# One load of seven rows in place of six rows and a row cut over 126 and 2 partitions, in a softmax kernel

## The chip, the cores and the metric

The kernel runs on one core of a Trainium2 chip. The metric is the device time in microseconds. The profile gives the span from the first to the last instruction, which is about 1.4 us shorter than the time.

## The reference

```python
x_scaled = x / 2.0                                   # x: 16 x 1024 x 512, float32
x_max = np.max(x_scaled, axis=-1, keepdims=True)
exp_x = np.exp(x_scaled - x_max)
return exp_x / np.sum(exp_x, axis=-1, keepdims=True)
```

So 16,384 rows of 2,048 bytes are read once and written once: 33.55 MB each way.

## The kernel before

Each of the 128 partitions gets 128 rows, in ten tiles of 3, 7, 13 and then seven times 15 rows. VectorE (DVE) takes the maximum of each row, ScalarE (ACT) the exponential with its sum, VectorE the reciprocal and the product, all in place in one arena. The first tile is loaded from SyncE's (SP) queue, all others from ScalarE's; the stores go out on SyncE's queue. I count tiles from 0 as the code does and call tile 1 the second tile, tile 2 the third.

```python
PLAN = [
    ([3], 0), ([4, 3], 3), ([5, 4, 4], 10), ([5] * 3, 23), ([5] * 3, 38), ([5] * 3, 53),
    ([5] * 3, 68), ([5] * 3, 83), ([5] * 3, 0), ([5] * 3, 15),
]
# ...
SPREAD = 1
# ...
FUSED = {1, 2, 3}
# ...
            if t == 0:
                nc.sync.dma_start(out=sb(t), in_=dram(xf, t)).then_inc(ld[t], 16)
            elif t == SPREAD:
                r = tiles[t][1] - 1
                for p, q, lo, hi in ((0, P, 0, r), (0, 126, r, r + 1), (126, P, r, r + 1)):
                    nc.scalar.dma_start(
                        out=sb(t)[p:q, lo:hi], in_=dram(xf, t)[p:q, lo:hi]
                    ).then_inc(ld[t], 16)
            else:
                nc.scalar.dma_start(out=sb(t), in_=dram(xf, t)).then_inc(ld[t], 16)
# ... (cut) the stores, one per tile, when its last product is done
        for t in range(len(tiles)):
            nc.sync.wait_ge(s_mul, last_chunk[t] + 1)
            nc.sync.dma_start(out=dram(of, t), in_=sb(t)).then_inc(
                st[t] if t in awaited else s_end, 16
            )
```

The second tile thus comes in three DMAs: six rows of all partitions, then the seventh row of partitions 0 to 125, then that of the last two. Below, *split* is this cut over 126 and 2 partitions. A *semaphore packet* is a 4-byte packet, which stands in the trace's packet strings after an engine's rows of a DMA. There are 336 here, which is 16 for each of 20 DMAs and 16 for the two of the split together. The second tile is waited for with 48 increments: 32 updates of its semaphore come from 7.35 us on, as many as its semaphore packets, and two updates at 1.30 and 1.65 us make up the rest. The *pair* are the two DMA engines whose strings hold no 2,048-byte packet, so no row of the split; the bytes that the pair is spared are its *relief*.

## Time and profile before

| | before |
|---|---|
| time, median of the first three runs | 160.04 us (159.99 to 160.07) |
| span of the profile | 158.6 us |
| DVE, ACT busy | 83%, 60% |
| DMA packets, moved | 3,026, 67.13 MB, mean 423 GB/s |
| landing of the second tile, third tile, last load | 9.25, 16.96, 127.64 us |
| issue of the last store, its landing | 146.98, 158.61 us |

How to read it: the 16 DMA engines have work all the time, while VectorE waits only for a handful of landings. The view of waits gives the whole idle time of VectorE for loads; the columns are total us, number of waits, longest.

```profile
DVE stats L118 <- DMA arena<-in_x_dram: 14.6, 5, 6.2
```

Four of these five waits matter here: for tiles 0, 1 and 2 (6.22, 1.30 and 2.37 us) and, near the end, for the last load (3.29 us).

### The profile page before, as it was taken

Reading aid. Unit: us, or ns where it says so; the run is one execution under the profiler, and the core shown is the slowest. Engines: PE = TensorE matmul, PEld = TensorE weight load, DVE = VectorE, ACT = ScalarE, POOL = GpSimd, SP = SyncE. Lnnn points to the kernel's source line nnn. Section 1 sums busy time; section 2 is a strip of 40 time slices with the busy share of each in tenths; the row PEclk is TensorE's granted clock in tenths of the full one; section 3 lists DMA queues with packets and bytes.
Section 4 is the critical chain, followed back from the end, with each engine's and each line's share of the span. In section 5 each row is a group of like instructions: output and inputs, shape, how many; then the busy total and the mean of one; then the engine's idle time right before and its main releaser. Section 6 shows DMA issues by size and latency. Waiting matters only on the chain.

```text
span 158.6 us, 621 instructions
## 1 busy us (share of the span) xinstructions
DVE 131.4 (83%) x155; ACT 94.4 (60%) x257; POOL 0.2 (0%) x4
## 2 busy tenths in 40 slices
DVE  0466799999999999999999999996999389999000
ACT  0369197736874594669738797666566809763000
POOL 0000000000000000000000000000000000000000
DMA  7999999999999999999999999999999999999996
GB/s 268 449 373 430 414 431 466 435 407 399 466 443 389 434 463 448 418 444 426 442 426 434 426 426 442 426 441 411 457 395 472 395 473 395 472 395 465 395 472 263
DMA packets 3026, 67.13 MB, mean 423 GB/s; under 512 B 336, under 2 KB 336, under 8 KB 720
## 3 DMA queue, kind: packets, MB, share of 16 engines
q1 hardware_dynamic: 1584, 34.34, 50.6%
q10 hardware_dynamic: 1440, 32.77, 48.5%
q14 instruction: 2, 0.02, 0.0%
HBM read 33.55 MB, written 33.55 MB: 423 GB/s over the span
## 4 chain that ended last, share of the span: by engine, by line
DMA 52%; DVE 38%; issue 0%
DMA arena<-in_x_dram 38%; DVE stats L118 18%; DMA out_dram<-arena 14%; DVE arena L131 13%; DVE arena L138 7%; DVE recip L127 1%
## 5 line engine op out<-in xcount | busy, mean ns | idle before, releaser
L118 DVE TENSOR_REDUCE stats<-arena 128x5 f32<-128x2560 f32 (+2 forms) x27 | 72.2, 2676 | 14.6 <-DMA arena<-in_x_dram 14.6
L176 ACT ACTIVATE arena<-arena,stats 128x512 f32<-128x512 f32 x68 | 48.2, 710 | 23.4 <-DVE stats L118 23.4
L211 ACT ACTIVATE arena<-arena,stats x60 | 42.5, 710 | 20.7 <-ACTq L203 20.7
L138 DVE TENSOR_SCALAR arena<-arena,recip 128x512 f32<-128x512 f32 x93 | 38.6, 482 | 0.7
L131 DVE TENSOR_TENSOR arena<-arena,recip 128x2560 f32<-128x2560 f32 (+2 forms) x8 | 19.9, 2491 | 0.3
L176 ACT ACTIVATION_READ_ACCUMULATOR arena<-arena,stats 128x1 f32 x68 | 12.7, 187 | 0.0
L211 ACT ACTIVATION_READ_ACCUMULATOR arena<-arena,stats x60 | 11.2, 187 | 0.0
L127 DVE RECIPROCAL recip<-stats 128x5 f32<-128x5 f32 (+2 forms) x27 | 4.8, 177 | 0.0
L171 ACT ACT_TABLE_LOAD x1 | 1.3, 1283 | 5.7 <-issue 5.7
L252 POOL MEMSET const-bfloat16-1.0<- 128x1 bf16 x1 | 0.1, 101 | 0.0
L252 POOL MEMSET const-uint8-127<- 128x1 uint8 x1 | 0.1, 101 | 0.0
L252 POOL MEMSET const-float32-0.0<- 128x1 f32 x1 | 0.1, 98 | 0.2 <-issue 0.2
L252 POOL MEMSET const-float32-1.0<- 128x1 f32 x1 | 0.1, 98 | 0.0
## 6 DMA issues: line engine op xcount, KB each, us to landing
arena<-in_x_dram ACTq DMA_DIRECT2D x7, 3840.0 KB, 46.6
out_dram<-arena SPq DMA_DIRECT2D x7, 3840.0 KB, 22.7
arena<-in_x_dram ACTq DMA_DIRECT2D x1, 3328.0 KB, 14.3
out_dram<-arena SPq DMA_DIRECT2D x1, 3328.0 KB, 21.1
out_dram<-arena SPq DMA_DIRECT2D x1, 1792.0 KB, 18.2
arena<-in_x_dram ACTq DMA_DIRECT2D x1, 1536.0 KB
arena<-in_x_dram SPq DMA_DIRECT2D x1, 768.0 KB, 6.2
out_dram<-arena SPq DMA_DIRECT2D x1, 768.0 KB, 15.8
```

The source lines that it names most:

```text
L118: nc.vector.reduce_max(out=stats[:, b : b + c], in_=arena[:, a : a + c], axis=mybir.AxisListType.X, negate=True,)._wait_ge(ld[t], 48 if t ...
L127: nc.vector.reciprocal(out=recip[:, b : b + c], in_=stats[:, b : b + c])._wait_ge(s_exp, k + 1).then_inc(s_rec, 1)
L131: nc.vector.tensor_mul(out=arena[:, a : a + c], in0=arena[:, a : a + c], in1=recip[:, b : b + c].unsqueeze(2).to_broadcast([P, c, D]),)._w ...
L138: ins = nc.vector.tensor_scalar_mul(out=arena[:, a + r], in0=arena[:, a + r], scalar1=recip[:, b + r : b + r + 1],)
L171: nc.scalar.preload_act_table(mybir.ActivationFunctionType.Exp)
L176: ins = nc.scalar.activation(out=arena[:, a + r], in_=arena[:, a + r], func=mybir.ActivationFunctionType.Exp, bias=stats[:, b + r : b + r ...
L211: ins = nc.scalar.activation(out=data, in_=data, func=mybir.ActivationFunctionType.Exp, bias=stat, scale=0.5, accum_out=stat,)
L252: nc = _bacc.Bacc("TRN2", target_bir_lowering=False, num_devices=1)
```

## The change

Its intent is to drop the special case: the second tile becomes one DMA of seven rows, with rows no longer dealt unevenly to the DMA engines.

```diff
-SPREAD = 1
...
-            elif t == SPREAD:
-
-                r = tiles[t][1] - 1
-                for p, q, lo, hi in ((0, P, 0, r), (0, 126, r, r + 1), (126, P, r, r + 1)):
-                    nc.scalar.dma_start(
-                        out=sb(t)[p:q, lo:hi], in_=dram(xf, t)[p:q, lo:hi]
-                    ).then_inc(ld[t], 16)
...
-        )._wait_ge(ld[t], 48 if t == SPREAD else 16).then_inc(s_max, 1)
+        )._wait_ge(ld[t], 16).then_inc(s_max, 1)
```

## The prediction

> **What bounds the kernel now.** I read the page first. VectorE (DVE) is the busiest compute engine at 83%, so it is no full bound, and ScalarE (ACT) at 60% is less. The row that matters is the DMA row of the 40 slices: nine tenths or more in every slice but the first and the last. In the queue table, q1 (the stores, and the first load) and q10 (all other loads) together fill 99.1% of sixteen engines' span.
>
> ```profile
> span 158.6 us, 621 instructions
> DVE 131.4 (83%) x155; ACT 94.4 (60%) x257; POOL 0.2 (0%) x4
> DMA  7999999999999999999999999999999999999996
> q1 hardware_dynamic: 1584, 34.34, 50.6%
> q10 hardware_dynamic: 1440, 32.77, 48.5%
> HBM read 33.55 MB, written 33.55 MB: 423 GB/s over the span
> ```
>
> The chain that ended last agrees only in part. It runs through DVE for 38% of the span, and that must not be taken as "DVE bounds it": the queues held enough work for the DMA engines while DVE was on the chain. Its start is what the change touches: the landing of the 13-row third tile at 16.96 us, then DVE without a pause.
>
> ```profile
> DMA 52%; DVE 38%; issue 0%
> 2.65 14.32 DMA arena<-in_x_dram
> 16.99 2.82 DVE stats L118
> 81.49 46.15 DMA arena<-in_x_dram
> 127.66 2.82 DVE stats L118
> ```
>
> Because DMA is full, the next question is which of the 16 engines ends last. The profile's views do not name the engine of a packet, but the trace has the start, duration, size and queue of each. A packet starts about 3.5 ns before the recorded end of the one before it on its engine, and each engine must see the same sequence (8 rows of each tile, then one 4-byte semaphore packet). With those two rules I joined all 3,024 data and semaphore packets into 16 gapless strings; the only pauses over 50 ns are two of 0.30 us, at the 8,192-byte instruction fetches at 28.1 and 71.3 us. This assignment is mine, an inference from times. Twelve strings contain nine 2,048-byte packets, two contain ten and two none, as the split demands. The two without are the last to end. What a window count can confirm of that: from 0 to 1.4 us 14 packets start, one on each of 14 engines; the other two engines start at 1.73 and 1.75 us. From 157.4 to 158.0 us 14 engines send their last semaphore packet; only from 158.05 us on do the last two.
>
> ```profile
> q1 hardware_dynamic: 14, 0.09, 35.5%
> ...
> q1 hardware_dynamic: 14, 0.00, 1.3%
> ...
> q1 hardware_dynamic: 2, 0.00, 0.5%
> ```
>
> (In order: windows 0 to 1.4, 157.4 to 158.0 and 158.05 to 158.3 us; the first figure is packets.) In my strings the fourteen engines with split rows end between 157.49 and 157.95 us, and the two without at 158.15 and 158.20. So the kernel ends when the two engines end that carry 18 KB less than the rest: 0.25 us after the next one, and 0.6 after most. They start about 0.5 us late and lose another half microsecond on stretched packets between 30 and 150 us.
>
> [...] the tile's semaphore got two early increments (1.30 and 1.65 us, by count the 2 + 14 that no engine sends) and 32 = 16 + 14 + 2 others from 7.35 to 9.25 us. [...] (from 18.3 us on, 6,144-byte stores alternate with 30,720-byte loads).
>
> **The change, part by part.**
>
> The view of issues by line has what goes:
>
> ```profile
> L110 ACTq DMA_DIRECT2D arena<-in_x_dram x3: 244/386/664, 0.1 to 1.2; - x3
> arena<-in_x_dram ACTq DMA_DIRECT2D x1, 252.0 KB
> arena<-in_x_dram ACTq DMA_DIRECT2D x1, 4.0 KB
> ```
>
> 1. Two issues on ACT's queue go: 3 x 431 ns on average become one, so about 0.9 us of sequencer time. They lie before the first ACT instruction that waits on data (8.01 us), and the next load is needed by an engine only when the second tile's packets are through (about 7.7 us). Worth nothing at the end.
> 2. Work of each engine. From the packet records: 12,288 B take 460 ns, 14,336 B take 535 (the stores of this very tile have that size), 2,048 B take 84, a semaphore packet 9; less the overlap of 3.5 each. Before, an engine of the fourteen spends 8 x 456.5 + 9 x 80.5 + 5.5 = 4,382 ns on this tile (its first semaphore packet is on both sides), the two that have the odd rows 86 more, and the last two 8 x 456.5 = 3,652. Afterwards all spend 8 x 531.5 = 4,252. So twelve engines save 0.13 us, two save 0.22, and the two slow ones get 0.60 more.
> 3. What lies on the path: the end is the maximum over engines. The fourteen fall to 157.3 to 157.8 us, which buys nothing. The two slow ones go from 158.15 and 158.20 to 158.75 and 158.80. The last landing was 0.42 us after the last semaphore packet (158.61), hence about 159.2: +0.60 us.
> 4. The tile lands earlier: without the burst of small packets, whose increments arrive up to 1.0 us after their packets, it should land near 8.40 + 0.45 = 8.85 us instead of 9.25 (0.45 is that delay at the third tile; 8.40 is the slow engines' 7.79 + 0.60). DVE waited 1.30 us there and waits 2.37 us again at 16.99 for the third tile, which comes 0.2 to 0.3 later. The early gain is swallowed by the later wait.
> 5. The tail on DVE: from the last load's landing (127.64) to the last store's issue (146.98) is 19.34 us. If the landing slips 0.6, so does the issue, to 147.6; with the 1.0 us from issue to first packet seen at the start, packets at 148.6. The slow engines finish the preceding store at 149.1 + 0.6, so they never starve; the quick ones may pause 0.3 us, inside their slack.
>
> Sum on the path: +0.60 us, all from step 3.
>
> **The rivals.**
>
> - *The late start comes from the split.* The two late engines start at 1.73 us, just after the last of ACT's three issues ended (1.48) and its immediate increments (1.65). If the three issues held up the first load's last two engines, removing them gives back up to 0.5 us and the time is about 160.15. For: the coincidence. Against: the first load is issued before all of them on another queue, and the two slow engines lose as much again after 30 us with no split in sight. I give it one in four.
> - *The gain in issues and in small packets counts.* If the fourteen engines set the end, the time would fall by 0.13 us to 159.9. Against: the last two semaphore packets are 0.2 us behind the rest, and 0.6 behind most.
> - *Changed order of traffic.* The first store may be issued about 0.4 us earlier and so interleave with other loads; with whole 30,720-byte packets (1.14 us) as the unit, landings can move by a packet. The store tail has 1.1 us of slack on the slow engines (149.1 against 148.0), so most of this stays hidden; if a landing slipped by two packets, 161.0 to 161.5 would come out.
> - *All DMA-bound engines even out.* If the stretched packets come from sharing with each other, a slower pair runs with fewer competitors at the end and regains some: +0.3, so 160.35.
>
> **Range and chances.** +0.60 is the plain sum, 160.64; the first and the last rival pull below it, the third above, and I take 160.6. The low end is the first rival (160.1), the high end a further half microsecond of stretched packets on the slow pair (161.1). Two per cent is 3.2 us, five times the effect, with runs of before within 0.1 us of each other: faster 1%, same 98%, slower 1%.
>
> **What would show it.** Right: 320 semaphore packets instead of 336 and no 2,048-byte ones (under 8 KB 576 = 320 + 256 instead of 720); one issue at that line; the same 14 packets before 1.4 us; 14 last semaphore packets at 157.3 to 157.9 us and two near 158.8; second tile's first reduction at 8.8 to 8.9 us and the third's near 17.2. Wrong: 16 packets before 1.4 us (first rival); the last semaphore packets within 0.3 us of each other; a DMA slice below nine tenths in the middle, or a wait of DVE after 130 us, which would mean that the order of traffic decides.

## The result

The changed kernel took 160.25 us (median of four runs, 159.98 to 160.38), the kernel before 160.06 in the same rounds (159.99 to 160.15). Executions over 1.5% slower than the fastest of the same kernel are left out of the means. Here and below a ratio is the mean time of one kernel's runs over that of the other's runs of the same rounds, so it is not quite the ratio of the medians quoted. It is 1.001, with a 95% interval of 0.9992 to 1.0027: no change that these runs can tell from zero, inside the predicted range, and well short of the +0.60 us of the sum.

The page of the changed kernel, lines that answer to those of before:

```profile
span 158.8 us, 619 instructions
DMA  7999999999999999999999999999999999999995
DMA packets 2882, 67.13 MB, mean 423 GB/s; under 512 B 320, under 2 KB 320, under 8 KB 576
```

The DMA row is as full as before. The packet counts are those predicted: 16 semaphore packets and 128 packets of 2,048 bytes are gone. Now the chain that ended last (start us, us, what):

```profile
1.59 14.86 DMA arena<-in_x_dram
...
16.47 2.82 DVE stats L110
...
81.33 46.90 DMA arena<-in_x_dram
...
128.25 2.82 DVE stats L110
```

Two starts are to be compared with those in the prediction. The third tile's reduction starts at 16.47 us instead of 16.99: 0.52 us earlier, where I had said 0.2 to 0.3 later. The last load's reduction starts at 128.25 instead of 127.66: 0.59 us later, as said. The gain of half a microsecond at 16 us is gone, and more, at 128 us. Where it goes is seen best in the windows view. Its columns are the window, its length, busy time and count of DVE, ACT and POOL, PE's clock, the DMA share, and GB/s by the packets that start in it. First before, then changed:

```profile
6.00:14.00 8.00, 6.44 (x6) 5.66 (x14) 0.00 (x0) 1.00 1.01 404
14.00:50.00 36.00, 33.42 (x21) 23.05 (x64) 0.00 (x0) 1.00 1.01 433
```

```profile
6.00:14.00 8.00, 7.06 (x7) 5.35 (x15) 0.00 (x0) 1.00 1.04 449
14.00:50.00 36.00, 33.30 (x21) 22.68 (x63) 0.00 (x0) 1.00 1.01 420
```

The share of busy DMA engines is full in all four; only the rate differs. Without the split the DMA engines move 449 GB/s between 6 and 14 us instead of 404, and then 420 instead of 433 for 36 us. As busy and moving less, the engines have stretched packets here; the table below has how much.

From the packets I rebuilt the sixteen strings again and took each engine's *lag*: the time of day less the time that its packets so far would have taken unstretched. Mean lag gained over the 16 engines, in us (not a view of the profile; the mean needs no strings, since the packets' times beyond the usual time of their size, summed and divided by 16, give the same within 0.04 us):

| kernel | 5 to 14 us | 14 to 60 us | 60 to 130 us |
|---|---|---|---|
| before | 0.56 | 0.30 | 0.06 |
| changed | 0.01 | 1.08 | 0.05 |

So the change takes away a stall of about half a microsecond on *all* engines near 8 us, which I had not expected, and gets as much and more back before 60 us. In the kernel before, 0.45 of the 0.56 us falls on 16 packets, the first of the third tile on each engine (1,341 to 1,485 ns where 987 is usual), and only 0.02 on the 2,048-byte packets themselves: the DMA that is cut looks normal, and the one behind it pays. What comes back has a place too. Between 14 and 25 us the engines lose, by the same sum, 0.36 to 0.51 us in each of the seven profiles of this text without an early stall, and 0.02 in each of the seven with one.

The window counts of the last semaphore packets (from 157.4 to 158.0, and from 158.05 to 158.3 us; the first figure is packets) answer to the 14 and 2 of before:

```profile
q1 hardware_dynamic: 10, 0.00, 0.9%
...
q1 hardware_dynamic: 5, 0.00, 1.1%
```

No pair stands alone any more: five engines end in the later window, and one more after it, at 158.44 us. The two engines that I took for last should have ended at 158.75 and 158.80.

### The profile page after: what moved, and what is told of

It reads as the page before. It is cut to its first block, busy times and chain, and to the rows that moved or that the text cites. A ratio compares the mean times of both kernels' runs of the same rounds, so it can differ in the third digit from the quotient of the medians.

```text
span 158.8 us, 619 instructions
## 1 busy us (share of the span) xinstructions
DVE 131.4 (83%) x155; ACT 94.4 (59%) x257; POOL 0.2 (0%) x4
## 4 chain that ended last, share of the span: by engine, by line
DMA 53%; DVE 38%; issue 0%
DMA arena<-in_x_dram 39%; DVE stats L110 18%; DMA out_dram<-arena 14%; DVE arena L123 13%; DVE arena L130 7%; DVE recip L119 1%
```

## The experiments

After the result I held three ideas against each other. *Burst*: the split's small packets stall all engines near 8 us. *Chance*: such stalls fall anywhere. *Pair*: the 0.60 us on two engines is real but hidden somewhere, or was never there. Twelve runs were made, in three batches of four; each batch shared its runs of the kernel before.

### The two kernels again

No edit.

> The kernel before against itself, to size chance. Theory 'burst' (the 126 + 2 small packets and their increments hold up all 16 engines by about 0.45 us near 8 us): the third tile lands again at 16.9 to 17.0 us and its first 26,624-byte packets take about 1,400 ns instead of 987. Theory 'chance' (pauses of this size fall anywhere, in both kernels): the landing is anywhere between 16.4 and 17.0, with pauses elsewhere than in the first profile. Both: ratio 1.000 within 0.001. The two engines without split rows again start last (1.7 us) and end last (158.1 to 158.3) by the pair theory.

> The changed kernel again. 'Burst': the third tile lands at 16.4 to 16.5 us as in its first profile, so the early 0.5 us is the change's own gain and cancels the 0.60 us of added work on the slow pair; time 160.1 to 160.4. 'Chance': landing anywhere from 16.4 to 17.0, and the time 160.25 in the mean because the pauses are spread over the engines differently; if the +0.60 of the prediction is real but masked in the first four runs, 160.5 to 160.7.

The kernel before, against itself: 160.14 us (160.01 to 160.50), ratio 1.0013 (0.9999 to 1.0026). The changed kernel: 160.07 us (159.96 to 160.36), ratio 1.0006 (0.9993 to 1.002). So the same program compared with itself differs by as much as the changed one did; at this size a ratio of 1.001 means nothing. The landing of the third tile, however, repeats: its reduction starts (start us, us, instruction, idle before it and what ended it) in the second profile of before and of changed at

```profile
17.10 2.82 DVE L118 TENSOR_REDUCE stats<-arena 128x5 f32<-128x2560 f32 x1 [2.47 <-DMA arena<-in_x_dram]
```

```profile
16.51 2.82 DVE L110 TENSOR_REDUCE stats<-arena 128x5 f32<-128x2560 f32 x1 [2.57 <-DMA arena<-in_x_dram]
```

Chance is out for the early stall: 0.58 us of mean lag from 5 to 14 us in the second profile of before, 0.05 in that of the changed kernel. The return of it repeats too: 0.27 and 0.95 us from 14 to 60.

These two profiles also raised the first doubt of my reading. In the second reconstruction of before, the two engines without split rows end at 157.49 and 157.60 us and others end last, at 158.25 and 158.13. Most engines keep a constant lag after 60 us, but two do not: one loses about 0.65 us at the 71 us fetch (0.30 idle, while 8,192 bytes take 309 ns, then a packet 0.35 longer), and one gains some 0.6 us of lag in small steps between 80 and 150. The first of these can be read without strings: in both profiles a packet of 1,488 ns, where 1,138 is usual, starts as the fetch ends. In my first reconstruction, both losses were partly on the strings of the pair.

### The odd row over all 128 partitions

```diff
-                for p, q, lo, hi in ((0, P, 0, r), (0, 126, r, r + 1), (126, P, r, r + 1)):
+                for p, q, lo, hi in ((0, P, 0, r), (0, P, r, r + 1)):
```

(and the wait for 32 instead of 48 increments)

> Second tile as 6 rows and then 1 row over all 128 partitions: the small packets stay (8 on each of 16 engines), the relief of the slow pair goes. 'Burst': the third tile lands at 16.9 to 17.1 us and, with 0.60 us more on the pair than before, the time is 160.5 to 160.8. 'Chance', or a burst that comes only from the 126 and 2 partition shapes: like the changed kernel, landing near 16.4 and time 160.1 to 160.4.

160.06 us (159.98 to 160.44), ratio 1.000 (0.9987 to 1.0014). It has as many small packets as the kernel before, and moves like the changed one:

```profile
6.00:14.00 8.00, 6.83 (x7) 5.42 (x15) 0.00 (x0) 1.00 1.06 448
14.00:50.00 36.00, 33.23 (x21) 22.66 (x65) 0.00 (x0) 1.00 1.00 423
```

The third tile landed at 16.77 us, between the two. Lag from 5 to 14 us: 0.17. So the burst of small packets makes at most a small part of the stall; my burst theory falls as it stood. Nor did the time rise by the 0.5 us or more that taking away the relief should have cost.

### Three rows over 126 and 2, over 128, and over 112 and 16

```diff
+                r = tiles[t][1] - 3
-                for p, q, lo, hi in ((0, P, 0, r), (0, 126, r, r + 1), (126, P, r, r + 1)):
+                for p, q, lo, hi in ((0, P, 0, r), (0, 126, r, r + 3), (126, P, r, r + 3)):
# three128:             ((0, P, 0, r), (0, P, r, r + 3)), and the wait for 32 increments
# three112:             ((0, P, 0, r), (0, 112, r, r + 3), (112, P, r, r + 3))
```

> Three rows of the second tile, not one, go over 126 and 2 partitions: the pair loses 1.2 us more work (8 packets of 6,144 B less), the fourteen gain 0.14. If the pair sets the end before: it now ends near 157.0, the others at 157.6 to 158.1, and the time is 159.8 to 160.0 (0.1 to 0.2 less than before). If late engines are just chance: 160.1 to 160.3, with another engine last. 'Burst' by number of packets (half the small ones' count is the same, 126 and 2 by 6,144 B): landing of the third tile still 16.8 or later; by their smallness: 16.5.

> 4 rows, then 3 rows over all 128 partitions. If the 1.0 us loss of 'three' comes from the number or size of its packets: third tile at 18 us or later, time near 161. If it comes from how 126 rows fall on 14 engines: third tile at 16.4 to 16.8, time 160.0 to 160.3.

> 4 rows, then 3 rows over 112 and 16 partitions. [...] If the loss comes from that fall of partitions: third tile at 17.3 to 18.6 and time 160.6 to 161.2. If it comes from having 14 engines only (14 of 16 lanes): like three128, third tile at 16.4 to 16.9 and time 160.0 to 160.3.

(The trace of this run has 352 semaphore packets, 16 for each of its 22 DMAs, so all 16 engines take part in the DMAs over 112 and over 16 partitions too. Shared evenly that is 7 rows and 1 row for each engine, where 128 partitions give 8: an estimate from these counts.)

The first was wrong in sign: 161.10 us (161.01 to 161.21), ratio 1.0066 (1.0052 to 1.0080). More relief for the pair made the kernel a microsecond *slower*. Over 128 partitions: 160.27 us (160.09 to 160.46), ratio 1.0005 (0.9989 to 1.0022). Over 112 and 16: 160.86 us (160.73 to 161.09), ratio 1.0051 (1.0034 to 1.0068). The windows of the three, in this order:

```profile
6.00:14.00 8.00, 4.44 (x3) 4.08 (x10) 0.00 (x0) 1.00 1.06 361
14.00:50.00 36.00, 33.45 (x24) 24.69 (x69) 0.00 (x0) 1.00 1.01 432
```

```profile
6.00:14.00 8.00, 6.64 (x7) 5.65 (x16) 0.00 (x0) 1.00 1.07 458
14.00:50.00 36.00, 33.20 (x22) 22.68 (x63) 0.00 (x0) 1.00 1.01 421
```

```profile
6.00:14.00 8.00, 4.98 (x3) 4.45 (x10) 0.00 (x0) 1.00 1.06 377
14.00:50.00 36.00, 33.19 (x24) 24.26 (x68) 0.00 (x0) 1.00 1.00 431
```

The rate between 6 and 14 us falls to 361 and 377 GB/s with the odd partition counts, and not with 128. All three have packets of 6,144 bytes for these rows, so size is out. The third has work on all 16 engines (the 352 semaphore packets above), so "14 of 16 engines" is out too. What is left is the number of partitions, and with it, by my inference, how they fall on the engines. Lag from 5 to 14 us: 1.73, 0.03 and 1.38 us; the first is about three times that of one row (0.56). One rival I did not test: the kernels that stall issue three DMAs for this tile, the others one or two. From one row over 126 and 2 to three rows the numbers of DMAs and of packets stay the same and the stall triples, which a cost for each DMA would not give; but no run has three DMAs of 128 partitions.

Why such a DMA stalls the engines was not shown: the traces do not name the engine of a packet, nor the partitions that an engine gets.

### The odd row over 112 and 16 partitions

```diff
+                for p, q, lo, hi in ((0, P, 0, r), (0, 112, r, r + 1), (112, P, r, r + 1)):
```

> The one odd row over 112 and 16 partitions, 16 engines each, so no relief for the pair. If the fall of partitions on the engines makes the stall: third tile at 16.8 to 17.1 us as before, no losses between 16 and 28 us, and 0.6 us more on the pair than before: time 160.2 to 160.7. If it needs 14 engines: third tile at 16.4 to 16.6, time 160.0 to 160.3.

159.91 us (159.88 to 159.98), ratio 0.9991 (0.9978 to 1.0005). The stall is there, as expected: 420 GB/s from 6 to 14 us, 428 from 14 to 50; third tile at 17.16 us, lag 0.50 and then 0.40. The time is not: I expected 0.1 to 0.6 us *more* than before, since the pair has no relief here (48 semaphore packets for this tile, 16 for each of its three DMAs), and it is the lowest median of all, though the interval does not part it from before. So a row kept from the pair is not what the kernel before lives on.

### The last store tagged

To see the pair at the end without following strings through 150 us, I cut the last store in the same way. In the tail only one queue has packets, and an engine that sends a semaphore packet after its share of the 14 rows and then no 2,048-byte packet must be one of the pair. (This takes it that the same cut spares the same engines in the second tile's load and in the last store.)

```diff
+            if t == len(tiles) - 1:
+                r = tiles[t][1] - 1
+                for p, q, lo, hi in ((0, P, 0, r), (0, 126, r, r + 1), (126, P, r, r + 1)):
+                    nc.sync.dma_start(
+                        out=dram(of, t)[p:q, lo:hi], in_=sb(t)[p:q, lo:hi]
+                    ).then_inc(s_end, 16)
+                continue
```

(and the last wait for 32 increments more)

> The kernel before, with the last store also cut into 14 full rows and one row over 126 and 2 partitions. This tags the two engines without odd rows at the end of the run itself, where only one queue is left and nothing can be confused. If my first reading holds (they end last, 0.25 us behind the next), their semaphore packets after the 14-row part are the two last of 16, at about 158.1 us less 0.6, and the time is 159.8 to 160.1. If my strings were swapped between like-timed engines in the middle, the two stand among the others or early there (their own lag 3.0 to 3.2 us less 0.73 of missing work is no more than the others' 2.3 to 2.9), other engines end last, and the time is 160.1 to 160.4.

> The changed kernel with the same cut in its last store. If the +0.60 us is real on the two engines but went into slack: they are now among the last three or four at the end of the 14-row part, level within 0.2 us with the engine that had the late instruction fetch, and 0.6 later relative to the others than in ls_before; time 159.9 to 160.3. If the +0.60 was never there: same rank as in ls_before. By my first reading: the last two by 0.8 us.

Times: 160.50 us (160.23 to 160.65), ratio 1.0022 (1.0005 to 1.0039), for the cut in the kernel before; 160.67 us (160.12 to 160.94), ratio 1.0024 (1.0000 to 1.0049), for that in the changed one; both ratios are to the kernel before. As kernels they gain nothing. As a measurement, of one profile each, they show where the pair stands. Start of the semaphore packet after the 14 rows, all 16 engines in order, the pair in brackets (from the packet records, us after 150):

```
cut in the kernel before:   6.88 6.90 [6.92] 6.95 7.02 7.03 [7.07] 7.11 7.12 7.16 7.21 7.32 7.46 7.62 7.83 8.00
cut in the changed kernel:  6.77 6.84 6.90 6.97 7.01 7.03 7.09 7.10 7.16 7.32 7.43 7.44 [7.55] 7.56 [7.82] 8.43
```

In the kernel before the pair is third and seventh of 16, a microsecond ahead of the last. In the changed kernel it is thirteenth and fifteenth, and the last is still 0.61 us behind it. The pair's mean against the median of the other fourteen moves from 6.995 - 7.14 = -0.14 to 7.685 - 7.09 = +0.59 us, that is by 0.73. The prediction's step 2 had 0.60 more for the pair and 0.13 less for the others: 0.73. So the extra work is real, in the size that was said (that the second digit agrees is chance: the two engines of the pair are 0.15 and 0.27 us apart); the place that I had given the pair in the order was wrong.

### The split on a later tile

```diff
-SPREAD = 1
+SPREAD = 4
```

> The 126 and 2 split on the last row of tile 4 (lands near 55 us), the second tile whole. If the stall of 0.46 us comes wherever the split is and only took the place of later losses when it came early: all engines lose it again near 55 us on top of the losses between 16 and 50, time 160.4 to 160.7. If the split stalls nothing when stores are mixed in: 160.0 to 160.2, with the pair early. Third tile at 16.4 to 16.5 in either case.

160.40 us (160.38 to 160.49), ratio 1.0022 (1.0008 to 1.0035). Tile 4 lands at 42.08 us, not near 55 as I wrote. The third tile landed at 16.43 us, as in the changed kernel. Packets near 40 us are stretched (0.21 us in the mean of the engines), half of what I expected. But the time is lost elsewhere. The last load's reduction comes a microsecond later than in the changed kernel,

```profile
129.25 2.82 DVE L118 TENSOR_REDUCE stats<-arena 128x5 f32<-128x2560 f32 x1 [3.29 <-DMA arena<-in_x_dram]
```

so the last store is issued at 148.56 instead of 147.57 us, and most engines run dry before each of the last two stores: by the packet records, 0.40 us in the mean of the engines near 140 and 0.16 near 149, where the changed kernel has none. Here the tail on VectorE sets the end. This is the third rival of the prediction (order of traffic). It says nothing about whether a stall after 50 us costs its full length.

### More VectorE work and fewer instructions

```diff
-FUSED = {1, 2, 3}
+FUSED = {1, 2, 3, 4, 5, 6}
```

> The changed kernel with tiles 4 to 6 scaled by one instruction per chunk as tiles 1 to 3 are: 36 VectorE instructions fewer, about 6.8 us more VectorE work in the middle, where it has idle time. If the fetch of 8,192 bytes at 71 us belongs to VectorE, it goes or moves (the page shows one packet on the instruction queue, or a later one), the 0.65 us that it costs one engine goes with it, and the last engine is another, near 158.2: time 0.1 to 0.3 below the changed kernel's 160.1 to 160.25. If the fetch stays at 71 us it is another engine's program, and the time does not change by more than chance, 0.2.

> The same edit on the kernel before. If the late fetch sets its end: without it the next ones end at 158.0 to 158.1, the time is 159.8 to 160.0 and it is equal or slightly below fuse6, because here the pair keeps its 0.6 us of slack and there it does not: fuse6 is 0.0 to 0.2 slower. If the fetch stays: no change beyond chance, 160.0 to 160.3.

On the changed kernel: 160.31 us (160.29 to 160.56), ratio 1.0015 (1.0001 to 1.0029). On the kernel before: 160.75 us (160.64 to 160.90), ratio 1.0042 (1.0028 to 1.0055). The fetch did not go; it moved from 71.5 to 76.4 us in one and from 71.3 to 78.2 in the other, so what it costs the end stays untested. But the pair of runs shows something else. VectorE waits for loads only three times, on the changed kernel and then on the one before:

```profile
DVE stats L110 <- DMA arena<-in_x_dram: 9.4, 3, 6.5
```

```profile
DVE stats L118 <- DMA arena<-in_x_dram: 9.9, 3, 6.3
```

These are the waits for tiles 0, 1 and 2; from the third tile's landing (16.45 and 16.97 us) VectorE runs to the end, and the last store is issued at 148.37 and 148.88. The 0.52 us at 16 us comes out as 0.51 us at the last store and 0.44 us in the median time. Before the last two stores the engines stand idle 0.43 us in the mean on the changed kernel and 0.98 on the one before. With VectorE as the bound, the changed load is worth 0.4 us; with DMA as the bound it is worth nothing.

## Why the prediction was right or wrong

**What bounds the kernel.** Right: the DMA engines, in both kernels, at 423 GB/s over the span.

**Which engines end last.** This is the step that failed ("the kernel ends when the two engines end that carry 18 KB less than the rest"). The joining of packets to strings by time is ambiguous where engines have like phases, and between 30 and 150 us strings must have been exchanged: the pair's strings took over losses that the later profiles put on others. The tagged store shows the pair 1.1 us and 0.9 us ahead of the last engine. With that falls the reading that two engines are slower: two start late (in the kernel before they send their first packet at 1.73 and 1.75 us, the others at 1.00 to 1.25), but no run shows them slower afterwards. That the window count also gave 14 and 2 at the end, as it does in the second profile of before, confirmed a count, not an identity; I had taken it for more.

**Step 1, the issues.** Right. The third tile is issued at 1.59 instead of 2.65 us, and no run shows anything at the end that follows from it.

**Step 2, the work.** Right: packet counts as stated, and 0.73 us between pair and rest, as measured in one pair of profiles.

**Step 3, the path.** Wrong, by the step above: +0.60 went into the pair's slack. With the change the pair stands among the late engines, 0.61 us before the last, so the change has used up a good part of that slack.

**Step 4, the landings.** The second tile landed at 8.53 us (8.85 said), the third at 16.44 (17.2 said). The missing term is a stall of about half a microsecond on all engines, made by a DMA over 126 partitions: 0.56 us of lag with the split, 0.01 with one DMA over 128. I had the sign of it before me, in first packets of the third tile of some 1,420 ns where 987 is usual, and gave it no term.

**Step 5, the tail.** Right in the length of the tail, and that no engine runs dry for long; the slip itself was a lucky hit. The last landing came 0.58 us later and the last store at 147.57 (147.6 said). But in the second pair of profiles the landing came 0.32 us later (127.72 and 128.04), and in the tagged pair 0.32 us *earlier* (128.02 and 127.70).

**The first rival.** Against it: in the changed kernel two packets still start at 1.73 and 1.75 us and take 474 and 455 ns where 234 is usual, like the two late first packets of before. The test that I had named (16 packets before 1.4 us) came out positive and was a bad one: three of the 16 were second packets.

**What the range owes to luck.** The measured 160.25 us lies in the range, but only near its low end, which I had put there for the first rival, and that did not come true; the same kernel's second median, 160.07, lies just below the range. The sum had one wrong term, +0.60 on an end that the pair does not set, and left out two that nearly cancel: a stall of 0.5 us that goes, and a loss that comes in its place. Lag from 14 to 60 us, in all 14 profiles, is 0.7 to 1.1 us where there was no early stall, 0.3 to 0.4 where it was about half a microsecond, and under 0.1 where it was 1.4 or more. So an early stall takes the place of later losses, and only what goes beyond them seems to be paid: three rows cost 0.8 to 1.1 us of time. Why the engines lose this time between 14 and 60 us, and why they lose none after, no run here settles.

Which engine ends last is also not fully settled; the one with the 71 us fetch is last in several reconstructions, and no run took that fetch away.

## What to carry to other kernels

When DMA is the bound, ask of each of its engines when it ends, and tag the engines in the part of the run where you need to know, with a shape that only some of them get, rather than follow strings through the whole run. A DMA over 126 or 112 partitions is not a cheap way to even out engines: it slowed all of them, by about half a microsecond per 2,048-byte row in the second tile and 0.21 us in a later one, and the relief of the pair bought no time that these runs can tell from zero. When such a stall is looked for, the packets of the next DMA are the place to look (0.45 of the 0.56 us here). And measure the kernel against itself before reading a ratio of 1.001.
